# A two-layer decoder trunk: sums at the entry of each FFN made by accumulating transfers, the last covered tiles finished in a given order, four covered tiles in the second FFN

## The chip, the cores and the metric

The kernel runs on one core of a Trainium2 chip. The metric is the device time of one launch in microseconds (us). Runs are compared on the same chip, and a verdict against the kernel before is given with an interval where several rounds were run.

The engines, as the profile names them: PE is the matrix engine (TensorE) and PEld its weight loads; DVE (VectorE) and ACT (ScalarE) work on tiles of 128 partitions; POOL (GpSimd) and SP (SyncE) issue transfers here. A transfer that POOL issues can add what it carries onto its target in SBUF ("accumulating transfer"); those of SP only copy.

## What is computed

A trunk of two layers over 512 tokens of width 1024, all in float32. The change concerns the two FFN of each layer, ffn1 and ffn2; the mixer between them is left alone.

```python
def swiglu(h, w_in, w_out):
    gate, up = jnp.split(h @ w_in, 2, axis=-1)
    return (jax.nn.silu(gate) * up) @ w_out
# per layer
x = x + 0.5 * swiglu(rms_norm(x, ffn1_norm), ffn1_w_in, ffn1_w_out)   # ffn1
x = x + mixer(rms_norm(x, mix_norm))
x = x + 0.5 * swiglu(rms_norm(x, ffn2_norm), ffn2_w_in, ffn2_w_out)   # ffn2
```

D = 1024, T = 512 tokens, and the hidden width is 2816, which is 22 tiles of 128. `w_in` holds 1024 x 5632 (gate, then up), `w_out` 2816 x 1024.

## The kernel before

Everything stands transposed: x as 8 tiles of 128 features x 512 tokens, weights as the held operand of the matmuls. Each float32 operand is split into a high and a low part ("hi", by a cast on ACT, and "lo", the rest, by a subtraction on DVE), and each product is made of three matmuls (hi·hi, hi·lo, lo·hi; `mm3`, L326, L332, L333).

**Two ways through `w_in`.** The hidden tiles are taken in pairs. The first few are "covered" (`cover`, L495): done plainly, 8 k-tiles x 4 banks x 3 matmuls of 128x512 = 96 for a pair. Their weights come in four granules per pair, which SP loads (L295) and ACT and DVE split (L314, L315). All others are done by a scheme of seven products instead of eight (`halved`, L637; a Strassen form): a unit is a pair of tiles, its weights in four quarters of 512x256 (q0, q1 the two halves of k for the gate, q2, q3 for up), x in four quarters, and each of the products P1 to P7 multiplies one combination of weight quarters with one combination of x quarters, in 24 matmuls of 128x256. The products of a unit run in the order P1, P2, P6, P5, P7, P3, P4; P1, P6, P7 and P4 accumulate onto one bank, which is copied out in between (g1 after P1, L792; g2 after P6, L799).

`covered` is 6 for ffn1 of layer 0, 4 for ffn1 of layer 1, and 6 for both ffn2 (in `trunk_kernel`, L1515 on). While the covered tiles run, everything that the first unit needs is made ready.

**The entry.** In the first covered pair the norm ends (`end_norm`, L426): `inv`, the inverse root of the mean square per token, exists then. `halves_of_x` (L576) scales x by it and by the gain (8 operations of 128x512 on DVE, L589), makes the sums of quarters that P6, P5, P7 and P4 need on DVE (L601, L607), and splits all seven parts (`part`, L614: ACT L620, DVE L621). It is a generator: two or seven parts are made during the first pair, the rest during the second.

The first unit's four quarters of weights are loaded into tiles of the pool that x's parts don't use, and DVE makes its four sums S1 to S4 (`total`, L685): S1 q2+q3, S2 = S, S3 = q0, S4 = q1. The first two are made before the covered tiles end, S3 and S4 during the first two products. For every later unit the first and the last sum are accumulating transfers on POOL (`add`, L672, from DRAM; `add_second`, L722, from the tile S). A product's weights are split three products ahead (`LEAD`, `prepare`, L687: ACT L697, DVE L699).

**What sets the order.** A scheduler orders what is not fixed; instructions passed to `follow` (L275; the short names A, V, G, S for ACT, DVE, POOL and SP) keep the order in which they are written on their engine. `plan` (L57) lists for every product which loads, sums and hidden sums are issued behind it.

**The last covered pair.** When it is done, its four banks hold gate and up of two tiles; `finish` (L547) multiplies them by `inv` (L552, L553), takes the SiLU (L269) and writes the hidden tiles (L571, L574). For the last pair this is done behind the first product (n == 0 in `ffn`, L449), in an order that the scheduler chooses.

Of the kernel before, what the change touches and what calls it, by code (L numbers as in the profile page):

```python
# [8 lines left out]
F32 = mybir.dt.float32  # L9
# [5 lines left out]
ALU = mybir.AluOpType  # L15
# [8 lines left out]
P = 128  # L24
# [25 lines left out]


SUM = {
    "P2": (1, 0), "P1": (0, 0), "P5": (0, 0), "P6": (0, 0), "P7": (0, 1), "P3": (1, 1), "P4": (0, 0),
# [3 lines left out]
def plan(covered):  # L57
# [34 lines left out]
    for u in dict.fromkeys((k, w) for k, w, _ in seq):  # L92
# [69 lines left out]
class Trunk:  # L162
# [273 lines left out]
    def ffn(self, w_in, w_out, next_gain, covered, begin=None, out=None):  # L436
# [5 lines left out]
        with tc.tile_pool(name=self.n("ffn"), bufs=1) as fp:  # L442
# [6 lines left out]
            for n, _ in enumerate(halved):  # L449

                if n == 0:
                    finish()

# [41 lines left out]
    def cover(self, fp, w_in, covered, begin, then):  # L495
# [7 lines left out]
        for f in range(0, covered, 2):  # L503
# [35 lines left out]
            def finish(f=f, banks=banks):  # L539
                for i in range(2):  # L540
                    self.finish(fp, f, i, banks[2 * i], banks[2 * i + 1])

            if f + 2 < covered:
                finish()
        return finish

    def finish(self, fp, f, i, pg, pu):  # L547
# [4 lines left out]
        nc.vector.tensor_mul(gi, pg, self.inv)  # L552
        nc.vector.tensor_mul(ui, pu, self.inv)  # L553
        self.act(gi, gi, AF.Silu)
        a, k = divmod(f + i, 4)
        for b in range(2):
            self.hidden(self.quarter(fp, 0, a, b)[:, k, :], *(t[:, 256 * b : 256 * b + 256] for t in (gi, ui)), a != b)

# [17 lines left out]
    def halves_of_x(self, fp):  # L576


        nc = self.nc
        H = T // 2  # L580
        xn = []
        self.ngain = self.const.tile([P, KD], F32, tag="ngain", name=self.n("ngain"))
        nc.scalar.activation(self.ngain, self.gain, AF.Copy, scale=-1.0)
        for q in range(4):
            xq = fp.tile([P, 2, T], F32, tag=f"r{q + 2}", name=self.n("xn"))
            for i in range(2):
                k = 2 * q + i

                nc.vector.scalar_tensor_tensor(  # L589
                    out=xq[:, i, :], in0=self.xT[:, k, :],  # L590
                    scalar=(self.ngain if k < 4 else self.gain)[:, k : k + 1],
                    in1=self.inv, op0=ALU.mult, op1=ALU.mult,
                )
            xn.append(xq)

        quarter = lambda a, b: [xn[2 * a + i][:, :, b * H : (b + 1) * H] for i in range(2)]
        both = lambda t: [t[:, 2 * i : 2 * i + 2, :] for i in range(2)]

        def minus(out, a, b, op=ALU.subtract):
            for o, u, v in zip(out, a, b):  # L600
                nc.vector.tensor_tensor(o, u, v, op=op)  # L601
            return out

        def neither(out, a, b):

            for o, u, v in zip(out, a, b):
                nc.vector.scalar_tensor_tensor(  # L607
                    out=o, in0=u, scalar=-1.0, in1=v, op0=ALU.mult, op1=ALU.subtract
                )
            return out  # L610

        self.xc = {}

        def part(name, src):  # L614
            c = len(self.xc)
# [3 lines left out]
            for h, l, u in zip(both(hi), both(lo), src):  # L619
                nc.scalar.copy(h, u)  # L620
                nc.vector.tensor_sub(l, u, h)  # L621
            self.xc[name] = hi, lo

        b11, b12, b21, b22 = (quarter(a, b) for a in range(2) for b in range(2))
# [12 lines left out]
    def halved(self, fp, w_in, w_out, covered):  # L637
# [63 lines left out]
        def moving(c, p):  # L701

            t = self.quarter(fp, c, *SUM[p])
# [3 lines left out]
            if p in ("P1", "P7", "P4"):  # L707
                A(nc.scalar.activation(hi, t, AF.Copy, scale=-1.0))
                V(nc.vector.scalar_tensor_tensor(
                    out=lo, in0=t, scalar=-1.0, in1=hi, op0=ALU.mult, op1=ALU.subtract  # L710
                ))
            else:
                A(nc.scalar.copy(hi, t))
                V(nc.vector.tensor_sub(lo, t, hi))
            mov[c, p] = hi, lo
# [27 lines left out]

        tags = {0: "03", 1: "51", 2: "42"}
        self.hh, self.hl = [], []
# [23 lines left out]
        for n, (kind, w, p) in enumerate(seq):  # L769
# [747 lines left out]
def trunk_kernel(  # L1517
# [6 lines left out]
    for l in range(DEPTH):  # L1524
# [41 lines left out]
```

## Time and profile before

| | us |
|---|---|
| median of 3 runs | 1871.98 |
| lowest, highest | 1868.59, 1883.21 |
| the profiled execution | 1880.58 |
| its span, first to last instruction | 1878.8 |
| mean granted clock of PE | 0.996 of full |
| PE busy | 1848.1 (98%) |
| DVE busy | 1480.0 (79%) |
| ACT busy | 1002.6 (53%) |
| POOL busy | 163.6 (9%) |

How the views read. A line of the timeline has the start, the duration, the engine, the line of the kernel, the operation, out<-in, the operand sizes, and in brackets how long the engine was idle before it and what released it. A list of waits has: who waits <- for whom: us in all, how often, longest. A window line has the stretch (us from the span's start), its length, the busy us and the number of instructions of each engine, the granted clock (1.00 is full), the share of DMA that was busy, and GB/s. "hl" are split weights, "xc" x's parts, "w" raw weights of a unit, "S" its sum, "st" a granule. The stages of the four FFN that matter, by the first weight load of each:

| | covered pairs | first product | g2 waited for at |
|---|---|---|---|
| ffn1, layer 0 | three | 81.4 | 95.19 |
| ffn2, layer 0 | 606.9, 629.5, 653.3 | 675.0 | 689.04 |
| ffn1, layer 1 | two, the last from 963.95 | 985.7 | 999.64 |
| ffn2, layer 1 | three | 1596.8 | 1610.05 |

### The profile page before, as it was taken

Reading aid. Unit: us, or ns where it says so; the run is one execution under the profiler, and the core shown is the slowest. Engines: PE = TensorE matmul, PEld = TensorE weight load, DVE = VectorE, ACT = ScalarE, POOL = GpSimd, SP = SyncE. Lnnn points to the kernel's source line nnn. Section 1 sums busy time; section 2 is a strip of 40 time slices with the busy share of each in tenths; the row PEclk is TensorE's granted clock in tenths of the full one; section 3 lists DMA queues with packets and bytes.
Section 4 is the critical chain, followed back from the end, with each engine's and each line's share of the span. In section 5 each row is a group of like instructions: output and inputs, shape, how many; then the busy total and the mean of one; then the engine's idle time right before and its main releaser. Section 6 shows DMA issues by size and latency. Waiting matters only on the chain. (4 is left out here: it accounts for less than half of the span.)

```text
span 1878.8 us, 33066 instructions
## 1 busy us (share of the span) xinstructions
PE 1848.1 (98%) x13384; PEld 1711.3 (91%) x13384; DVE 1480.0 (79%) x2117; ACT 1002.6 (53%) x1483; POOL 163.6 (9%) x170
## 2 busy tenths in 40 slices
PE   8999999999999999999999999999999999999999
PEld 6899999899878789999889999988998777999997
DVE  7978886677887868879687887867768878787783
ACT  4455554564676535555455555545547663545552
POOL 0011120100000001112000111201000000020210
PEclk9999999999999999999999999999999999999999
DMA  5658783232323367868255786813223235577762
GB/s 146 179 137 190 181 179 91 73 92 68 79 79 96 100 172 176 182 169 169 79 155 149 168 190 170 169 62 93 81 65 86 80 99 156 159 148 189 150 131 90
DMA packets 241513, 245.60 MB, mean 131 GB/s; under 512 B 19504, under 2 KB 226864, under 8 KB 241360
## 3 DMA queue, kind: packets, MB, share of 16 engines
q1 hardware_dynamic: 191792, 183.69, 32.2%
q0 software_dynamic: 49568, 59.79, 19.9%
q8 instruction: 105, 1.72, 0.4%
q14 instruction: 48, 0.39, 0.1%
HBM read 220.83 MB, written 2.10 MB: 119 GB/s over the span
## 5 line engine op out<-in xcount | busy, mean ns | idle before, releaser
L697 ACT CAST hl<-w 128x1024 fp32r<-128x1024 f32 x310 | 325.0, 1049 | 352.1 <-PE mm L333 94.1
L699 DVE TENSOR_TENSOR hl<-w,hl 128x1024 fp32r<-128x1024 f32 x310 | 378.6, 1222 | 103.3 <-ACT hl L697 103.0
L326 PE MATMUL mm<-xc,hl 128*128 128x256 f32 (+1 forms) x1011 | 282.6, 280 | 6.9 <-ACT g L799 6.9
L333 PE MATMUL mm<-xc,hl 128*128 128x256 f32 x1008 | 282.3, 280 | 0.0
L332 PE MATMUL mm<-xc,hl 128*128 128x256 f32 x1008 | 282.1, 280 | 0.0
L315 DVE TENSOR_TENSOR hl<-st,hl 128x512 fp32r<-128x512 f32 (+2 forms) x204 | 176.4, 866 | 114.9 <-ACT hl L314 113.6
L314 ACT CAST hl<-st 128x512 fp32r<-128x512 f32 (+2 forms) x204 | 154.9, 762 | 192.8 <-PE mm L333 65.7
L326 PEld LDWEIGHTS mm<-xc,hl 128*128 128x128 f32 x1011 | 192.0, 190 | 7.8 <-ACT g L799 7.5
L333 PEld LDWEIGHTS mm<-xc,hl 128*128 128x128 f32 x1008 | 192.7, 191 | 0.2
L332 PEld LDWEIGHTS mm<-xc,hl 128*128 128x128 f32 x1008 | 191.7, 190 | 0.0
L326 PE MATMUL mm<-hl,x 128*128 128x256 f32 (+1 forms) x384 | 112.6, 293 | 0.7 <-DVE ft L420 0.4
L326 PE MATMUL mm<-x,hl 128*128 128x512 f32 x272 | 109.2, 401 | 0.0
L333 PE MATMUL mm<-hl,x 128*128 128x256 f32 (+1 forms) x384 | 107.7, 281 | 0.0
L332 PE MATMUL mm<-hl,x 128*128 128x256 f32 (+1 forms) x384 | 107.5, 280 | 0.0
L333 PE MATMUL mm<-x,hl 128*128 128x512 f32 x272 | 106.5, 391 | 0.0
L332 PE MATMUL mm<-x,hl 128*128 128x512 f32 x272 | 106.0, 390 | 0.0
L333 PE MATMUL sc<-m,hl 128*128 128x256 f32 x336 | 93.6, 279 | 0.0
L332 PE MATMUL sc<-m,hl 128*128 128x256 f32 x336 | 93.4, 278 | 0.0
L326 PE MATMUL sc<-m,hl 128*128 128x256 f32 x336 | 93.4, 278 | 0.0
L326 PE MATMUL po<-xc,hl 128*128 128x256 f32 x336 | 93.4, 278 | 0.0
L332 PE MATMUL po<-xc,hl 128*128 128x256 f32 x336 | 93.4, 278 | 0.0
L333 PE MATMUL po<-xc,hl 128*128 128x256 f32 x336 | 93.4, 278 | 0.0
(474 smaller groups left out, 5515.8 us busy)
## 6 DMA issues: line engine op xcount, KB each, us to landing
w<-in_ffn_w_in_dram SPq DMA_DIRECT2D x132, 512.0 KB, 5.1
w<-in_ffn_w_out_dram SPq DMA_DIRECT2D x64, 512.0 KB, 4.4
w<-in_ffn_w_out_dram POOLq DMA_DIRECT2D x56, 512.0 KB, 8.4
st<-in_ffn_w_in_dram SPq DMA_DIRECT2D x88, 256.0 KB, 3.1
st<-in_w_mix_in_dram SPq DMA_DIRECT2D x88, 256.0 KB, 2.7
w<-in_ffn_w_in_dram POOLq DMA_DIRECT2D x29, 512.0 KB, 8.1
w<-S POOLq DMA_DIRECT2D x29, 512.0 KB, 4.8
st<-in_ffn_w_out_dram SPq DMA_DIRECT2D x24, 512.0 KB, 3.5
```

Of the source, the lines that this page charges most:

```text
L314: a = nc.scalar.copy(hi, src[:, c : c + w])
L315: b = nc.vector.tensor_sub(lo, src[:, c : c + w], hi)
L326: i = nc.tensor.matmul(acc[:, c], ah, bh[:, c], start=first and c.start == 0, stop=False, skip_group_check=True,)
L332: nc.tensor.matmul(acc, ah, bl, start=False, stop=False, skip_group_check=True)
L333: i = nc.tensor.matmul(acc, al, bh, start=False, stop=last, skip_group_check=True)
L697: A(nc.scalar.copy(hi, src))
L699: return lambda: V(nc.vector.tensor_sub(lo, src, hi))
```

## The change

1. *x's sums.* `halves_of_x` scales x by quarters (16 operations of 128x256 in place of 8 of 128x512), and the sums of quarters are made by four accumulating transfers on POOL, SBUF to SBUF: a: (0,0)+=(0,1), b: (0,1)+=(1,1), c: (0,0)+=(1,1), d: (0,0)+=(1,0), of 512 KB each. The signs that DVE's subtractions had are put into the gain and into the split (`two`, for `NEGATIVE`). Each part is split in one piece of 128x1024. The parts come in the order P1, P2, P3, P5, P6, P7, P4.
2. *The first unit.* Its quarters are loaded by SP in the order q2, q0, q3, q1 into tiles of their own, and a fifth load puts q2 into S as well. POOL then adds q3 onto q2, q0 onto S and q3 onto S; q0+=q2 and q1+=S come later, as for other units. The four sums on DVE are gone.
3. *The last covered pair* is finished one tile behind the second product and one behind the fourth, in the given order. Its gate tile uses the buffers of g2 instead of g1. `halved` yields once more, so that the loads go ahead of the last pair but one.
4. *Small ones.* g1 is now g1 - acc (the sign moved), and one Square is put in the order of the activation tables.
5. *ffn2 has four covered tiles* instead of six, so one more unit of the seven products.

```diff
+NEGATIVE = ("P1", "P7", "P4")
...
             if w == covered:
-                begin = {0: -5, 1: -4, 2: -3, 3: -2}
-                when(-1, 9, "total", u, "S1")
-                when(-1, 9, "total", u, "S2")
-                when(0, 2, "total", u, "S3")
-                when(1, 2, "total", u, "S4")
+                when(-1, 5, "add", u, 0, 2)
+                when(-1, 6, "adds", u)
+                continue
...
-        nc.scalar.activation(t, r, AF.Square)
+        self.act(t, r, AF.Square)
...
-                if n == 0:
-                    finish()
+                if n in (1, 3):
+                    finish(n // 2)
...
-            if f + 2 == covered:
+            if f + 4 == covered or f + 2 == covered:
                 next(then)
...
-        gi = fp.tile([P, T], F32, tag="g1", name=self.n("gi"), bufs=2)
+        gi = fp.tile([P, T], F32, tag="g2", name=self.n("gi"), bufs=2)
...
+        A, V = ((lambda i, e=e: self.follow(e, i)) if keep else (lambda i: i) for e in "av")
+        V(nc.vector.tensor_mul(gi, pg, self.inv))
+        V(nc.vector.tensor_mul(ui, pu, self.inv))
+        A(self.act(gi, gi, AF.Silu))
...
-        yield part("P1", b11)
-        yield part("P2", b21)
-        t1 = both(fp.tile([P, 4, H], F32, tag="S", name=self.n("T"), bufs=2))
-        minus(t1, b12, b11)
-        t2 = minus(b11, b22, t1, ALU.add)
-        yield part("P6", t2)
-        yield part("P5", t1)
-        yield part("P7", neither(b12, b12, b22))
-        yield part("P3", b22)
-        yield part("P4", minus(b21, b21, t2))
+        add = lambda x, y: nc.gpsimd.dma_start(q(*x), q(*y), accum_op=ALU.add)
...
+        yield part("P1")
+        add((0, 0), (0, 1))
+        yield part("P2")
+        yield part("P3")
+        yield part("P5")
+        add((0, 0), (1, 1))
+        add((0, 1), (1, 1))
+        yield part("P6")
+        add((0, 0), (1, 0))
+        yield part("P7")
+        yield part("P4")
...
-        first = [x for x in steps[-1] if x[0] == "total"]
-        steps[-1] = [x for x in steps[-1] if x[0] != "total"]
-        run(-1)
+        u = seq[0][:2]
+        for q in (2, 0, 3, 1):
+            raw[u, q] = t = fp.tile(
+                [P, 4, 2 * P], F32, tag=("mh", "ml")[q % 2], name=self.n("w"), bufs=2
+            )
+            S(nc.sync.dma_start(t, src(u, q)))
+        sums[u] = fp.tile([P, 4, 2 * P], F32, tag="S", name=self.n("S"), bufs=2)
+        S(nc.sync.dma_start(sums[u], src(u, 2)))
+        add(u, 2, 3)
+        for q in (0, 3):
+            G(nc.gpsimd.dma_start(sums[u], src(u, q), accum_op=ALU.add))
+        yield
         for s in seq[: LEAD - 1]:
             prepare(*s)()
+        run(-1)
         yield
-        for _, args in first:
-            total(*args)
         prepare(*seq[LEAD - 1])()
...
-                V(nc.vector.tensor_add(g1, g1, acc))
+                V(nc.vector.tensor_sub(g1, g1, acc))
...
         k.ffn(
-            ffn2_w_in[l], ffn2_w_out[l], ffn1_norm[l + 1] if l + 1 < DEPTH else None, 6,
+            ffn2_w_in[l], ffn2_w_out[l], ffn1_norm[l + 1] if l + 1 < DEPTH else None, 4,
```

In the built kernel POOL's order at each entry is q2+=q3, S+=q0, S+=q3, a, b, c, and then, in ffn2, q0+=q2, q1+=S, d, and in ffn1 d, q0+=q2, q1+=S. In ffn2 SP's five loads stand behind the third granule of the last covered pair. ACT has the split of P4's x part ahead of the g1 copy.

More of the change, by code (lines that the diff above doesn't have):

```diff
@@ L618, in part, with two @@
             )
-            for h, l, u in zip(both(hi), both(lo), src):
-                nc.scalar.copy(h, u)
-                nc.vector.tensor_sub(l, u, h)
+            self.two(hi, lo, src, name in NEGATIVE)
             self.xc[name] = hi, lo
-        b11, b12, b21, b22 = (quarter(a, b) for a in range(2) for b in range(2))
-        yield part("P1", b11)
-        yield part("P2", b21)
-        t1 = both(fp.tile([P, 4, H], F32, tag="S", name=self.n("T"), bufs=2))
-        minus(t1, b12, b11)
-        t2 = minus(b11, b22, t1, ALU.add)
-        yield part("P6", t2)
-        yield part("P5", t1)
-        yield part("P7", neither(b12, b12, b22))
-        yield part("P3", b22)
-        yield part("P4", minus(b21, b21, t2))
+        yield part("P1")
[9 more added lines that the diff above has]
+        yield part("P4")
+    def two(self, hi, lo, src, other):
+        nc = self.nc
+        if other:
+            return (
+                nc.scalar.activation(hi, src, AF.Copy, scale=-1.0),
+                nc.vector.scalar_tensor_tensor(
+                    out=lo, in0=src, scalar=-1.0, in1=hi, op0=ALU.mult, op1=ALU.subtract
+                ),
+            )
+        return nc.scalar.copy(hi, src), nc.vector.tensor_sub(lo, src, hi)
     def halved(self, fp, w_in, w_out, covered):
@@ L701, in moving @@
         def moving(c, p):
-            t = self.quarter(fp, c, *SUM[p])
             hi, lo = (
@@ L706, in moving @@
             )
[L707 to L714, printed above, removed]
+            a, v = self.two(hi, lo, self.quarter(fp, c, *SUM[p]), p in NEGATIVE)
+            A(a), V(v)
             mov[c, p] = hi, lo
@@ L742, in halved @@
         pair = lambda t: t.rearrange("p (i t) -> p i t", i=2)
-        tags = {0: "03", 1: "51", 2: "42"}
+        tags = {0: (0, 3), 1: (5, 1), 2: (4, 2)}
         self.hh, self.hl = [], []
@@ L750, in run @@
                 do[name](*args)
-        first = [x for x in steps[-1] if x[0] == "total"]
-        steps[-1] = [x for x in steps[-1] if x[0] != "total"]
-        run(-1)
+        u = seq[0][:2]
+        for q in (2, 0, 3, 1):
+            raw[u, q] = t = fp.tile(
+                [P, 4, 2 * P], F32, tag=("mh", "ml")[q % 2], name=self.n("w"), bufs=2
+            )
+            S(nc.sync.dma_start(t, src(u, q)))
[5 more added lines that the diff above has]
+        yield
         for s in seq[: LEAD - 1]:
             prepare(*s)()
+        run(-1)
         yield
-        for _, args in first:
-            total(*args)
         prepare(*seq[LEAD - 1])()
```

50 lines of the change are left out of this document (18 added, 32 removed).

## The prediction

> **What bounds the kernel now.** I read the busy shares first, then the list of waits of TensorE's weight loads, then the instructions around the waits that stand alone, and last the busy time by stretches.
>
> ```profile
> span 1878.8 us, 33066 instructions
> PE 1848.1 (98%) x13384; PEld 1711.3 (91%) x13384; DVE 1480.0 (79%) x2117; ACT 1002.6 (53%) x1483; POOL 163.6 (9%) x170
> PEld mm L326 <- ACT g L799: 7.5, 3, 2.9
> PEld sc L326 <- ACT xc L620: 3.7, 2, 1.8
> PEld sc L326 <- ACT g L799: 2.8, 1, 2.8
> ```
>
> PE is busy 98% of the span, so only three things move the time: matmuls fewer or more, idle gaps of PE, and the clock it is granted. The rows of the waits read: who waits, for whom, us in all, how often, longest. The g2 copy (L799) makes four gaps, one at each FFN's entry; the split of x (L620) makes two, in the two ffn2. These six are what the change touches. Here is ffn2 of layer 0: weight loads, then the two other engines, then stretches (from:to, length, busy us of PE, PEld, DVE, ACT, POOL with instruction counts, granted clock, DMA share, GB/s).
>
> ```profile
> 651.27 0.19 PEld L333 LDWEIGHTS po<-x,hl 128*128 128x128 f32 x1
> 653.30 0.19 PEld L326 LDWEIGHTS sc<-x,hl 128*128 128x128 f32 x1 [1.84 <-ACT xc L620]
> 674.99 0.19 PEld L326 LDWEIGHTS mm<-xc,hl 128*128 128x128 f32 x1
> 686.00 0.19 PEld L333 LDWEIGHTS mm<-xc,hl 128*128 128x128 f32 x1
> 689.04 0.19 PEld L326 LDWEIGHTS mm<-xc,hl 128*128 128x128 f32 x1 [2.86 <-ACT g L799]
> ```
> ```profile
> 687.45 1.04 ACT L697 CAST hl<-w 128x1024 fp32r<-128x1024 f32 x1 [2.30 <-DVE w L685]
> 688.40 0.59 ACT L799 ACTIVATE g<-mm 128x512 f32<-128x512 f32 x1
> 686.15 1.22 DVE L685 TENSOR_TENSOR w<-w,S 128x1024 f32<-128x1024 f32 x1
> ```
> ```profile
> 653.30:675.00 21.70, 21.67 (x96) 17.95 (x97) 13.46 (x22) 6.28 (x9) 1.34 (x1) 1.00 0.67 203
> 675.00:685.90 10.90, 10.90 (x97) 10.86 (x96) 10.31 (x15) 5.45 (x7) 0.00 (x0) 1.00 0.65 178
> 686.00:693.27 7.27, 4.61 (x27) 4.41 (x26) 3.82 (x4) 2.97 (x4) 0.00 (x0) 0.77 0.51 159
> 689.50:693.00 3.50, 3.50 (x19) 3.50 (x18) 1.48 (x2) 0.93 (x2) 0.00 (x0) 0.51 0.52 163
> ```
>
> A covered pair takes 21.70. Four products take 10.90, so one takes 2.72 and a pair in seven products 19.1. The fifth product waits for g2, which stands on ACT behind a weight split, which waited for the first unit's last sum on DVE (686.15 to 687.37). It takes 7.27 where 2.72 are due: 4.55 lost, of it 2.86 waiting and 1.7 because the clock stood at 0.51 for 3.5 us behind the wait (3.5 x 0.49). Behind the shorter wait at 651.27 the next 96 matmuls ran at clock 1.00, so a gap of 1.84 costs itself only (2.03 from load to load).
>
> **The change part by part.** *Four covered tiles in ffn2.* Per ffn2 21.70 - 19.1 = 2.6 of PE go, and the wait at 653.30, which stood ahead of the third pair, must be looked for elsewhere: the products now begin at 651.3, when they are ready, instead of 675.0. *First unit's sums off DVE.* S1 to S4 leave DVE, and so does what made g2 late. The other entries:
>
> ```profile
> 95.19 0.19 PEld L326 LDWEIGHTS mm<-xc,hl 128*128 128x128 f32 x1 [2.61 <-ACT g L799]
> 999.64 0.19 PEld L326 LDWEIGHTS sc<-xc,hl 128*128 128x128 f32 x1 [2.77 <-ACT g L799]
> 1610.05 0.19 PEld L326 LDWEIGHTS mm<-xc,hl 128*128 128x128 f32 x1 [2.06 <-ACT g L799]
> ```
>
> With 1.7 of clock each they are worth 4.3 (ffn1, layer 0), 4.5 (ffn1, layer 1) and 3.8 (ffn2, layer 1). The price of 1.7 rests on a clock that halves after waits of this length; the Trainium skill ("TensorE: Matmul & The Clock Gate", Part 1 on the clock gate) puts the limit at idle gaps above some 3.4 us. The stretch at 0.51 after a wait of 2.86 contradicts that; by the page the four waits were worth their 10.3 alone, not 17.2, and the sum would come out 7 higher at the entries and lower where I charge new waits.
>
> *What takes their place.* The queue of POOL now carries, per entry: q2+=q3, S+=q0, S+=q3, the four sums of x (a to d), q0+=q2, q1+=S. In ffn2 the order is q2+=q3, S+=q0, S+=q3, a, b, c, q0+=q2, q1+=S, d; in ffn1 a to d stand ahead of the last two. S+=q3 waits until S+=q0 has landed, and everything behind waits with it. The rows for such transfers: issues on POOL, then from issue to landing.
>
> ```profile
> 105.33 0.90 POOL L722 DMA_DIRECT2D w<-S  x1 [31.08 <-DVE hl L699]
> 105.88 1.67 POOL L672 DMA_DIRECT2D w<-in_ffn_w_in_dram  x1
> ```
> ```profile
> w<-S POOLq DMA_DIRECT2D x1, 512.0 KB, 4.7
> w<-in_ffn_w_in_dram POOLq DMA_DIRECT2D x1, 512.0 KB, 7.6
> ```
> ```profile
> w<-in_ffn_w_in_dram POOLq DMA_DIRECT2D x29, 512.0 KB, 8.1
> w<-S POOLq DMA_DIRECT2D x29, 512.0 KB, 4.8
> ```
> ```profile
> DMA to landing us min/median/max: 5.5/8.2/15.0
> ```
> ```profile
> DMA to landing us min/median/max: 4.5/4.8/6.3
> ```
>
> The two last are for L672 (from DRAM) and L722 (from SBUF). The pair at 105 lands at 110.0 and 113.5: a transfer issued right behind another comes about 3.3 later. I take 7.6 for one from DRAM that starts alone, 4.8 for one from SBUF, 3.3 for one behind another; ends 5.5 and 8.4, 4.5 and 6.3. 7.6 because the entries are full of weight loads; the third pair's stretch shows the load:
>
> ```profile
> GB/s 0 59 203 413 164 0 0 0 39 231 374 226 205 300 238 180 247 280 347 339 162 252 334 385 392 279 293 300 297 138 141 195 206 180 175 254 300 313 367 303
> w<-in_ffn_w_in_dram POOLq DMA_DIRECT2D x1, 512.0 KB, 8.4
> ```
>
> *ffn2, layer 0.* When can the five loads of the first unit start? They stand on SP behind a wait for DVE's last squared-sum addition (L414), 622.54 + 0.68:
>
> ```profile
> 622.54 0.68 DVE L414 TENSOR_TENSOR sqa<-sqa,sq 128x512 f32<-128x512 f32 x1
> L697 ACT CAST hl<-w 128x1024 fp32r<-128x1024 f32 x310 | 325.0, 1049 | 352.1 <-PE mm L333 94.1
> L699 DVE TENSOR_TENSOR hl<-w,hl 128x1024 fp32r<-128x1024 f32 x310 | 378.6, 1222 | 103.3 <-ACT hl L697 103.0
> 682.47 0.42 DVE L571 SCALAR_TENSOR_TENSOR hq<-gi,ui 128x256 f32<-128x256 f32 x1
> 683.74 0.68 DVE L552 TENSOR_TENSOR gi<-pt,inv 128x512 f32<-128x512 f32 x1
> ```
>
> Five of 0.52 MB at some 290 GB/s (an estimate from the busy slices above) and two us of way: S lands at 635. S+=q0 635 to 642.6; S+=q3, issued 0.5 later, 650.7; copy a 3.3 behind it, about 654. Then P5's x part: ACT 1.05, DVE 1.22, 656.3. DVE's queue holds two hidden tiles and a product behind that (2 x 0.42 + 0.68), then P1's weight split (1.22): 659. The first product is due at 651.3 and starts at 659: 7.7 late. ACT's queue is behind the same part, and has the copies for P7, P6 and P4 of x ahead of the g1 copy; P6 accumulates onto P1's bank and so needs that copy. Copy c, which waits for P5's split, lands at 662.4; q0+=q2, which waits for P1's split, 659.3 to 666.9; q1+=S 3.3 later, copy d another 3.2: 673.3. P4's part 1.05, a weight split 1.05, g1 0.59: 676. P6, the third product, runs 676 to 680.6 (2.72 + 1.7 for the clock), and should have ended at 651.3 + 3 x 2.72 = 659.5: 21.1 late. After that everything has landed. So this entry takes 21.1 + 19.1 = 40.2 from 651.3, against 2.0 + 21.7 + 4.55 = 28.3 before: **+11.9**. In layer 1, with 27.5 before, **+12.7**.
>
> *ffn1, layer 1.* Here are four covered tiles before and after, and the last pair ran
>
> ```profile
> 963.95:985.70 21.75, 21.75 (x98) 18.01 (x97) 21.75 (x35) 10.94 (x17) 1.32 (x1) 1.00 0.76 215
> 947.61 0.69 DVE L414 TENSOR_TENSOR sqa<-sqa,sq 128x512 f32<-128x512 f32 x1
> ```
>
> The loads go at 948.3, S lands at 960 (11.7 as above), the two sums at 967.6 and 975.7, copy a at 978.9. ACT has P5's part ahead of the split of the last of the pair's four granules; with a SiLU between and DVE's 1.22 that granule is ready at 984, due at 985.7 - 21.75/4 = 980.3. Lost: 3.7 + 1.7. Copy c waits for P5's split and d for P6's, a transfer of 4.8 and two splits each: d lands at 995, P4's part and P2's weights behind it (1.05 + 1.05 + 1.22) let the second product start at 998.7, 4.6 after the first (991.4 + 2.72) ended: lost 4.6 + 1.7. Together 11.7 against the 4.5 that go: **+7.2**.
>
> *ffn1, layer 0.* The same order, but the weights come in the kernel's first 20 us and x is whole far ahead of the products; I find every transfer landing before the entry: **-4.3**.
>
> *The rest at nothing.* Sixteen scalings of x at 0.42 for eight at 0.68 add 1.3 to DVE under a covered pair, where it is idle most (13.46 of 21.70). The last pair's finish in two halves is hidden under seven products, since their banks are other ones; if it were not, it costs its 0.68 twice. The sign of g1 and the place of one Square change no duration.
>
> Sum: 11.9 + 12.7 + 7.2 - 4.3 = **+27.5**. The profiled execution, 1880.6 us with its span of 1878.8, would become 1908; the median of the three runs is 1872, and 1872 + 27.5 is some **1900**.
>
> **The rivals.** *The transfers meet little traffic* (5.6 from DRAM, 3.2 behind). For: ffn2 loads fewer granules than before in this stretch. Against: five loads more, and 8.4 in the stretch quoted. Sums at 640.6 and 646.7, a at 649.9, first product 654.9, q0+=q2 660.9, d 667.3, g1 670, P6's end 674.5, 15 late: +5.8 and +6.5; in ffn1, layer 1, copy a is in time and only P2 waits, about 7.4, +2.9; with -4.3 it is +11: 1883.
>
> *All transfers cost like the lowest from SBUF*, 4.5, as if the source and the accumulation counted for nothing: sums 639.5 and 644.5, a 647.7, first product some 1.5 late, c 654.5, P6's split 658.8, d 663.3, g1 666: 9.3 + 1.7 late, +1.8 and +2.5; ffn1, layer 1, -2; in all -2: 1870. Against it: 5.5 is the lowest of the transfers from DRAM. The Trainium skill ("DMA: Bandwidth & Descriptors", "Anatomy of one DMA — SWDGE (gpsimd) path") goes further, 2.0 us and the bytes at 436 GB/s, 3.2 for 512 KB, by which I would estimate about 1860; no transfer of the trace is that short.
>
> *All is ahead of the products* (the faster side). Then four waits (4.55 + 4.5 + 4.3 + 3.8) and in each ffn2 2.03 and 2.6 go: -26.4, 1846. It decides at copy a landing by 645 and d by 653, that is with loads that start some 10 us earlier than the addition at 622.54 lets them.
>
> *Worse*: at 8.4 and 6.3 throughout, the chain of five in ffn2 is some 7 longer, +44 in all: 1916.
>
> **How the numbers follow.** Chances: forecast 0.56, worse 0.05, little traffic 0.23, lowest rows 0.08, all ahead 0.08. One per cent, about what a measurement here can tell, is 18.7 us: slower by that are the forecast and the worse, 0.61; within it the two next, 0.31; faster 0.08. The forecast's own range by the bounds of the transfers is 1890 to 1914; down to 1874 it takes in the case of little traffic and leaves out lowest rows, all ahead and half of the worse, under 0.2.
>
> **What would show it.** Right: in both ffn2 a wait of PE ahead of the first product of 5 to 9 us and one ahead of the third of 10 to 16, with ACT's P4 part of x or the g1 copy as releaser; no wait at L799; S+=q3 landing near 650 and copy d near 673; the clock at half behind each. In ffn1, layer 1, a wait inside the last covered pair and one at the second product. Wrong: if S+=q3 lands before 643, or if the g1 copy does not stand behind copy d, nearly all of the +25 of the two ffn2 is gone.

## The result, and the profile after

| | median of 4 runs, us | lowest, highest |
|---|---|---|
| before | 1870.28 | 1864.67, 1883.21 |
| after | 1933.88 | 1917.16, 1943.38 |

The ratio is 1.032, 95% interval 1.023 to 1.041: slower, by 63.6 between the medians where 27.5 was forecast. The profiled execution after took 1933.97 against 1880.58, 53.4 more. First the head of the page after and its waits of the weight loads (who waits <- for whom: us in all, how often, longest):

```profile
span 1932.2 us, 33422 instructions
PE 1862.2 (96%) x13528; PEld 1730.9 (90%) x13528; DVE 1456.8 (75%) x2077; ACT 1009.3 (52%) x1467; POOL 206.9 (11%) x210
```
```profile
PEld sc L334 <- DVE hl L698: 21.6, 3, 10.9
PEld sc L327 <- ACT g L792: 16.3, 2, 8.3
PEld mm L327 <- ACT hl L696: 9.8, 3, 5.1
```

Line numbers have moved: L327 and L334 are the first and the third matmul of a split product, L698 and L696 the low and high split of weights, L792 the g1 copy, L600 the copies a to d, L754 the sums onto S. The g2 copy is gone from the list, and the six old waits with it. Three groups stand in their place, in the order of the lines: the first product of each ffn2 waits for P1's weights, its third for g1, and in both ffn1 the second product for P2's weights. Here are the first two in ffn2 of layer 0, from the timeline of the weight loads:

```profile
673.89 0.29 PEld L334 LDWEIGHTS sc<-xc,hl 128*128 128x128 f32 x1 [10.87 <-DVE hl L698]
689.95 0.29 PEld L327 LDWEIGHTS sc<-xc,hl 128*128 128x128 f32 x1 [7.98 <-ACT g L792]
```

Behind them, POOL's queue (start, duration of the issue), the time from issue to landing of its transfers (last number; the two onto S, a, and d, in their order), and ACT:

```profile
644.77 1.28 POOL L754 DMA_DIRECT2D S<-in_ffn_w_in_dram  x1 [3.72 <-DMA S<-in_ffn_w_in_dram]
655.23 1.29 POOL L754 DMA_DIRECT2D S<-in_ffn_w_in_dram  x1 [9.18 <-DMA S<-in_ffn_w_in_dram]
655.98 1.46 POOL L600 DMA_DIRECT2D xn<-xn  x1
680.09 0.86 POOL L600 DMA_DIRECT2D xn<-xn  x1 [0.25 <-DVE xc L634]
```
```profile
S<-in_ffn_w_in_dram POOLq DMA_DIRECT2D x1, 512.0 KB, 10.2
S<-in_ffn_w_in_dram POOLq DMA_DIRECT2D x1, 512.0 KB, 10.9
xn<-xn POOLq DMA_DIRECT2D x1, 512.0 KB, 13.1
xn<-xn POOLq DMA_DIRECT2D x1, 512.0 KB, 7.3
```
```profile
669.13 1.04 ACT L634 CAST xc<-xn 128x1024 fp32r<-128x1024 f32 x1 [16.04 <-DMA xn<-xn]
687.41 1.06 ACT L629 ACTIVATE xc<-xn 128x1024 fp32r<-128x1024 f32 x1 [8.43 <-DMA xn<-xn]
688.37 1.03 ACT L696 CAST hl<-w 128x1024 fp32r<-128x1024 f32 x1
689.31 0.59 ACT L792 ACTIVATE g<-sc 128x512 f32<-128x512 f32 x1
```

The chain can be read off: the second sum starts when the first has landed (644.77 + 10.2), copy a stands behind it and lands at 669.1, ACT sits idle for 16 us in front of P5's part, and everything queued behind that part is late. Then the same once more with d, P4's part and g1.

A second thing is in no list of waits. Stretches of 20 us in the middle of the products (length, busy us of PE, PEld, DVE, ACT, POOL with counts, clock, DMA share, GB/s), after:

```profile
150.00:170.00 20.00, 20.00 (x172) 20.00 (x171) 18.76 (x21) 10.59 (x12) 4.84 (x5) 1.00 0.82 167
740.00:760.00 20.00, 20.00 (x179) 20.00 (x178) 15.65 (x17) 8.99 (x11) 3.53 (x3) 1.00 0.54 119
```

PE is busy throughout and its clock is 1.00 in both, yet 172 matmuls fall into one and 179 into the other (the two or three that overlap the edges counted in): from start to start it is about 118 ns ("the longer step" from here on) against 113.4. One rate holds from one wait to the next. After, both ffn1 ran at the longer step nearly to their end, 8.7 and 9.5 us each; before, ffn2 of layer 1 did, 8.4, and the tail of ffn1 of layer 0.

So that the two are kept apart, the steps from one weight load to the next are summed by FFN, over the products and the 26 us ahead of them: what exceeds 113.4 ns (226.7 in covered pairs) counts as a wait when the step is over 400 ns, as half clock between 170 and 400, and as the longer step below 170.

| us: wait, half clock, longer step | before | after |
|---|---|---|
| ffn1, layer 0 | 2.7, 2.0, 0.9 | 4.5, 2.6, 8.7 |
| ffn2, layer 0 | 4.7, 1.9, 0.0 | 19.0, 4.5, 0.1 |
| ffn1, layer 1 | 3.2, 1.8, 0.0 | 12.0, 3.1, 9.5 |
| ffn2, layer 1 | 3.9, 1.6, 8.4 | 19.4, 4.3, 1.0 |
| waits and half clock, sum | 21.8 | 69.4 |
| longer step, sum | 9.3 | 19.3 |

Waits and half clock +47.6, longer steps +10.0, matmuls saved 5.3 (21.70 - 19.05 in each ffn2): +52.3 of the 53.4.

### The profile page after: what moved, and what is told of

The parts are those of the page before. It is cut to its first block, busy times and chain, and to the rows that moved or that the text cites. A ratio compares the mean times of both kernels' runs of the same rounds, so it can differ in the third digit from the quotient of the medians.

```text
span 1932.2 us, 33422 instructions
## 1 busy us (share of the span) xinstructions
PE 1862.2 (96%) x13528; PEld 1730.9 (90%) x13528; DVE 1456.8 (75%) x2077; ACT 1009.3 (52%) x1467; POOL 206.9 (11%) x210
## 4 chain that ended last, share of the span: by engine, by line
PE 82%; DMA 7%; DVE 5%; ACT 3%; issue 3%; POOL 0%; SPq 0%; ACTq 0%; POOLq 0%; DVEq 0%
PE mm L327 12%; PE mm L334 12%; PE mm L333 12%; PE sc L327 6%; PE sc L333 6%; PE sc L334 5%; PE pt L327 5%; PE pt L333 5%; PE pt L334 5%; DMA xn<-xn 3%; PE po L327 3%; PE po L333 3%; PE po L334 3%; DMA S<-in_ffn_w_in_dram 1%; DVE hl L316 1%
## 5 line engine op out<-in xcount | busy, mean ns | idle before, releaser
L696 ACT CAST hl<-w 128x1024 fp32r<-128x1024 f32 x322 | 337.5, 1049 | 346.8 <-PE mm L334 93.9
L698 DVE TENSOR_TENSOR hl<-w,hl 128x1024 fp32r<-128x1024 f32 x322 | 393.3, 1222 | 101.9 <-ACT hl L696 101.3
L327 PE MATMUL mm<-xc,hl 128*128 128x256 f32 (+1 forms) x730 | 207.7, 285 | 8.9 <-ACT hl L696 8.9
L334 PE MATMUL mm<-xc,hl 128*128 128x256 f32 x728 | 207.8, 285 | 2.6 <-DVE hl L698 2.6
L333 PE MATMUL mm<-xc,hl 128*128 128x256 f32 x728 | 207.4, 285 | 0.0
L334 PE MATMUL sc<-xc,hl 128*128 128x256 f32 x528 | 150.3, 285 | 21.0 <-DVE hl L698 21.0
L327 PE MATMUL sc<-xc,hl 128*128 128x256 f32 (+1 forms) x530 | 150.2, 284 | 15.9 <-ACT g L792 15.9
L327 PEld LDWEIGHTS mm<-xc,hl 128*128 128x128 f32 x730 | 141.3, 194 | 9.8 <-ACT hl L696 9.8
L333 PE MATMUL sc<-xc,hl 128*128 128x256 f32 x528 | 149.7, 284 | 0.0
L334 PEld LDWEIGHTS mm<-xc,hl 128*128 128x128 f32 x728 | 139.5, 192 | 3.4 <-DVE hl L698 3.4
L333 PEld LDWEIGHTS mm<-xc,hl 128*128 128x128 f32 x728 | 141.2, 194 | 0.0
L327 PE MATMUL pt<-xc,hl 128*128 128x256 f32 x480 | 132.6, 276 | 0.0
L333 PE MATMUL pt<-xc,hl 128*128 128x256 f32 x480 | 132.6, 276 | 0.0
L334 PE MATMUL pt<-xc,hl 128*128 128x256 f32 x480 | 132.6, 276 | 0.0
L334 PEld LDWEIGHTS sc<-xc,hl 128*128 128x128 f32 x528 | 103.2, 195 | 21.6 <-DVE hl L698 21.6
L327 PEld LDWEIGHTS sc<-xc,hl 128*128 128x128 f32 x530 | 103.6, 195 | 16.4 <-ACT g L792 16.3
L327 PE MATMUL mm<-hl,x 128*128 128x256 f32 (+1 forms) x384 | 112.2, 292 | 0.7 <-DVE ft L421 0.4
L327 PE MATMUL mm<-x,hl 128*128 128x512 f32 x272 | 109.8, 404 | 0.0
L334 PE MATMUL mm<-hl,x 128*128 128x256 f32 (+1 forms) x384 | 107.3, 279 | 0.0
```

What stands on the lines that cost most here:

```text
L327: i = nc.tensor.matmul(acc[:, c], ah, bh[:, c], start=first and c.start == 0, stop=False, skip_group_check=True,)
L333: nc.tensor.matmul(acc, ah, bl, start=False, stop=False, skip_group_check=True)
L334: i = nc.tensor.matmul(acc, al, bh, start=False, stop=last, skip_group_check=True)
L696: A(nc.scalar.copy(hi, src))
L698: return lambda: V(nc.vector.tensor_sub(lo, src, hi))
```

## The experiments

The same sums, and the medians, for all of them. "Ratio" is against the kernel before on the same chip (its medians there 1874 to 1877).

| | median, us | ratio (95%) | waits and half clock | longer step |
|---|---|---|---|---|
| e1 after, six covered | 1904.04 | 1.013 (1.007 to 1.019) | 24.9 | 18.1 |
| e2 after, x on DVE | 1882.40 | 1.002 (0.999 to 1.005) | 29.3 | 19.3 |
| e3 before, four covered | 1878.09 | 1.000 (0.997 to 1.004) | 29.9 | 18.4 |
| e4 before, given order | 1880.44 | 1.003 (0.9995 to 1.006) | 14.0 | 17.7 |
| e5 after, S on DVE | 1903.97 | 1.015 (1.010 to 1.020) | 50.8 | 9.9 |
| e6 after, P4 late | 1912.93 | 1.021 (1.017 to 1.025) | 60.1 | 9.2 |
| e7 before, g2 first | 1864.40 | 0.994 (0.992 to 0.997) | 7.7 | 9.1 |
| e8 after again | 1924.47 | 1.026 (1.022 to 1.030) | 69.4 | 9.8 |
| e9 after, held loads | 1928.51 | 1.027 (1.020 to 1.034) | 67.2 | 10.7 |
| e10 after, x on DVE, six | 1855.86 | 0.988 (0.982 to 0.994) | 5.3 | 0.9 |
| e11 as e10, g2 and u2 first | 1870.86 | 0.995 (0.991 to 0.998) | 4.1 | 9.7 |
| e12 before, g2 and u2 first | 1858.98 | 0.989 (0.984 to 0.994) | 5.9 | 0.7 |

The account closes: 1871.3 (the profiled execution before without its longer steps), plus the change of both columns, less 5.3 where four tiles are covered in ffn2, gives each profiled time within 1.3 us; for e1, with the 11.6 of its covered pairs added, within 2.1.

**e1, six covered tiles in ffn2.**

```diff
-            ffn2_w_in[l], ffn2_w_out[l], ffn1_norm[l + 1] if l + 1 < DEPTH else None, 4,
+            ffn2_w_in[l], ffn2_w_out[l], ffn1_norm[l + 1] if l + 1 < DEPTH else None, 6,
```

> The changed kernel with six covered tiles in ffn2 again; all else as changed. In the changed kernel's trace S+=q3 lands 3 to 4 us behind the due time of the first product of ffn2, copy d 20 behind it. Theory 1, the chain of transfers is too long for four covered tiles: with 21.7 us more ahead of the first product the two waits of ffn2 (10.9 and 8.0 of PE, clock 4.4 beside) fall to below 3 us each, 2.6 of matmuls come back per ffn2: 1934 - 47 + 5, some 1892. Rival, the waits hang on the order on ACT and DVE and move along with the products: ffn2 keeps over 12 us of waits, 1925 or more. Either way each FFN that ends its last wait at a step of 118 ns from matmul to matmul instead of 113.4 has 8 to 9 us more, so one such stage up or down moves these figures by 9.

Median 1904, 12 above the first theory's 1892. The waits of 10.9 and 8.0 went, as that theory says. But in the second covered pair of each ffn2 some 5.8 us of waits came up; weight loads and DVE there:

```profile
669.82 0.29 PEld L327 LDWEIGHTS pt<-x,hl 128*128 128x128 f32 x1 [5.11 <-DVE ui L555]
```
```profile
667.94 1.23 DVE L630 SCALAR_TENSOR_TENSOR xc<-xn,xc 128x1024 fp32r<-128x1024 f32 x1 [3.81 <-ACT xc L629]
669.08 0.68 DVE L555 TENSOR_TENSOR ui<-pt,inv 128x512 f32<-128x512 f32 x1
```

In DVE's queue the split of a part of x (L630), which waits for a copy, stands ahead of the read of a bank (L555) that PE wants for the next pair, and that read starts only behind it. The copies do harm even where the cover is long.

**e2, x's sums on DVE.** The part `halves_of_x` is that of the kernel before. P2's part has the other sign then, and its product is subtracted as in the changed kernel, so one term of the gate has the wrong sign; the instructions and their shapes are the same. With the copies go the split of each part in one piece and the new order of the parts; the three were not tried apart.

> The changed kernel with x's sums on DVE as before (halves_of_x of the kernel before); the first unit's sums stay transfers, four covered tiles stay. Theory 1, the copies a to d make most of the waits: ffn2's wait at the first product (10.9) and at the third (8.0) fall together below 7 per ffn2, the third product now waiting for S+=q3 alone; ffn1 of layer 0 has no wait over 1 us, ffn1 of layer 1 less than 4 of its 12: about 1890. Rival, the sums onto S are to blame alone: the third product waits for S as long as now and the first still over 5, 1915 or more. Second rival, DVE is too full with x's sums when only four tiles are covered: a wait of over 8 us for DVE ahead of the first product, 1915 or more.

Median 1882: 42 to 52 less than the changed kernel. ffn1 of layer 0 has no wait left. In ffn2 the first product waits little, and the second, P2, whose weights are S, waits for the split of S (the third was expected to):

```profile
648.07 0.29 PEld L334 LDWEIGHTS sc<-xc,hl 128*128 128x128 f32 x1 [2.46 <-DVE hl L713]
658.96 0.28 PEld L334 LDWEIGHTS sc<-xc,hl 128*128 128x128 f32 x1 [6.67 <-DVE hl L713]
```

More than the 7 in sum that was expected (9.1 and 10.9), and the profiled execution, 1891.9, has 19.3 of longer steps in it; without them it would lie at 1873, where the kernel before would lie at 1871. So the copies of x, with what is queued behind them, make most of the loss; the sums onto S are late by themselves in ffn2 with four covered tiles, and e10 below shows no such wait with six.

**e3, four covered tiles alone**, in the kernel before, by the same edit as e1's in the other direction.

> The kernel before with four covered tiles in ffn2 and nothing else of the change. If the four covered tiles are worth their matmuls, 2 x 2.6, and the sums on DVE come in time: 1865. If DVE, busy 21.73 of 21.80 us in the second pair, can't have x's parts and the first unit's sums ready 21.7 us earlier: waits of 3 to 8 us at the first products of each ffn2, 1872 to 1885. If any kernel with four covered tiles waits as the changed one does: 19 us of waits per ffn2, 1900 or more.

Median 1878, ratio 1.000: the middle case. A wait of 3.7 for the split of P1's weights on DVE at the first product eats the matmuls saved and the old bank wait.

**e4, the finish in the given order alone**, in the kernel before: the edit of the diff above in `ffn`, `cover` and `finish`.

> The kernel before with the last covered pair finished in two halves behind the second and the fourth product, in the given order, and nothing else of the change. The wait for g2 (2.06 to 2.86 us at four entries, 10.3 in all, and 1.7 each at half clock) stands behind DVE's fourth sum. If that sum is late because the finish of the last pair is ahead of it on DVE: all four waits below 1 us, 1870 - 13 to 17, some 1855, and since no wait is left every product at 113.4 ns a matmul. If the sum is late for another reason (S3, the splits): waits as before, 1870 within 5.

Median 1880, 3 above the kernel before: no gain, and the second case comes nearest. g2 still waits, but partly for something new: ACT, and the weight load that it lets go:

```profile
683.11 0.63 ACT L269 ACTIVATE gi<-gi 128x512 f32<-128x512 f32 x1 [2.50 <-DVE gi L553]
```
```profile
685.22 0.19 PEld L326 LDWEIGHTS mm<-xc,hl 128*128 128x128 f32 x1 [1.88 <-ACT g L800]
```

The order puts a SiLU of the covered tile, which waits for DVE, ahead of the g2 copy. The waits are a little shorter and cost hardly any half clock (14.0 for 21.8), but in the profiled execution both ffn2 were left at the longer step, which took as much again.

**e5, S made on DVE**, x's sums still transfers.

```diff
-        S(nc.sync.dma_start(sums[u], src(u, 2)))
         add(u, 2, 3)
-        for q in (0, 3):
-            G(nc.gpsimd.dma_start(sums[u], src(u, q), accum_op=ALU.add))
         yield
+        total(u, "S2")
```

> The changed kernel with the first unit's S made by one addition on DVE (S = q0 + (q2+q3), 1.22 us) in place of the fifth load and the two accumulating transfers; x's sums stay transfers, four covered tiles stay. Theory 1, the transfers S+=q0 and S+=q3, each waiting for the one before, are what holds copy a back to 669: a then stands behind q2+=q3 alone, lands some 12 to 18 us earlier, the wait of 10.9 at ffn2's first product falls below 2, and the one of 8.0 at the third below 5, since d comes earlier too; ffn1 of layer 1 loses its wait inside the covered pair: 1890 to 1900. Rival, the four copies of x are too long by themselves: over 12 us of waits are left per ffn2, 1915 or more.

Median 1904, 20 to 30 less than the changed kernel, between the two cases. Copy a landed at 657.7 instead of 669.1, 11 earlier; the waits in ffn2 of layer 0 fell to

```profile
669.52 0.29 PEld L334 LDWEIGHTS sc<-xc,hl 128*128 128x128 f32 x1 [6.52 <-DVE hl L698]
681.09 0.29 PEld L327 LDWEIGHTS sc<-xc,hl 128*128 128x128 f32 x1 [4.47 <-ACT g L789]
```

not below 2. Copy a itself now waits for the split of P1's part on DVE and starts at 649.3, so the chain of S was only part of its lateness. And a is no longer what the first product waits for: it landed some 5 us before that product began. On DVE the split of P1's weights (L698) now stands behind that of P7's part (L630), which waits for the next copy, b:

```profile
665.35 1.06 ACT L629 ACTIVATE xc<-xn 128x1024 fp32r<-128x1024 f32 x1 [5.54 <-DMA xn<-xn]
666.44 1.23 DVE L630 SCALAR_TENSOR_TENSOR xc<-xn,xc 128x1024 fp32r<-128x1024 f32 x1 [4.02 <-ACT xc L629]
668.25 1.22 DVE L698 TENSOR_TENSOR hl<-w,hl 128x1024 fp32r<-128x1024 f32 x1
```

**e6, P4's part behind g1.**

```diff
+                if n == 0:
+                    for _ in self.xparts:
+                        pass
...
+            a, v = self.two(hi, lo, src, name in NEGATIVE)
+            if name == "P4":
+                self.follow("a", a)
+                self.follow("v", v)
```

> The changed kernel with the part P4 of x split behind the first product's g1 copy, in the given order on ACT and DVE; every transfer stays where it is. Theory 1, what waits in the entry is not P4's product (the seventh) but the work queued behind P4's part on ACT: the waits at P2 in ffn1 go (3.2 + 1.05 in layer 0, 5.1 + 0.96 in layer 1, and 2.6 and 3.1 of clock), the one at the third product of ffn2 (8.0) falls below 3, where S itself is waited for; the one at the first product (10.9, copy a) stays: 1934 - 28 to 38. Rival, the products wait for the late copies anyway: new waits at the fourth to seventh products, 1925 or more.

Median 1913, between the two cases. The six other parts are made ahead, and `xparts` has P4's left. In ffn1 of layer 0 waits and half clock fell from 7.1 to 2.3, and in ffn2 the third product no longer waits for g1. But two products on there is a wait of the same size (weight load, and ACT before it):

```profile
679.71 0.29 PEld L327 LDWEIGHTS sc<-xc,hl 128*128 128x128 f32 x1 [7.32 <-ACT g L805]
```
```profile
672.92 1.06 ACT L635 ACTIVATE xc<-xn 128x1024 fp32r<-128x1024 f32 x1 [6.89 <-DMA xn<-xn]
679.07 0.59 ACT L805 ACTIVATE g<-sc 128x512 f32<-128x512 f32 x1
```

P4's part still waits for copy d in ACT's queue, now ahead of g2. Both theories had a share: the queue makes the wait, and moving the part hands it to the next in the queue.

**e7, the g2 copy first**, in the kernel before.

```diff
+            if n == 2:
+                work[u, "g2"] = g2 = tmp("g2")
+                A(nc.scalar.activation(g2, acc, AF.Copy, scale=-1.0))
             rest = prepare(*seq[n + LEAD]) if n + LEAD < len(seq) else None
...
+            elif p == "P6" and n == 2:
+                pass
```

> The kernel before with one instruction moved: in the first unit of each FFN the copy of g2 stands ahead of the split of P3's weights on ACT instead of behind it. If g2 waits only for its place behind that split (which waits for DVE's fourth sum): the four waits of 2.06 to 2.86 and the 1.7 each at half clock are gone, -13 to -17 against the kernel before, and with no wait left inside the products every stage runs at 113.4 ns a matmul, which saves the 8 to 9 us of a stage that a wait left at 118: 1850 to 1862. If P3's weights are late themselves: a wait of 0.5 to 2 us two products later, -5 to -10.

Median 1864, 10 less than before. The four waits went; 0.4 to 1.0 came at the sixth product, not for P3's weights as the second case had it, but for u2. One of these left ffn1 of layer 0 at the longer step.

**e8, the changed kernel again.**

> The changed kernel once more, unchanged. In its first profile the products ran at 118 ns from matmul to matmul in both ffn1 (8.7 and 9.5 us in all) and at 113.4 in both ffn2, and changed between the two only at a wait. If a wait leaves it at one or the other by chance: the same waits within 0.5 us, but another set of slow stages, and a time of 1915 and 8 to 9.5 for each slow stage. If code or addresses decide: the same two stages, 1934 within 3.

Median 1924. Waits and half clock sum to 69.4 as before, single waits within 1.2, but the longer step is in another place; stretches of this run:

```profile
150.00:170.00 20.00, 20.00 (x179) 20.00 (x179) 19.19 (x20) 10.90 (x12) 5.93 (x5) 1.00 0.88 171
1700.00:1720.00 20.00, 20.00 (x172) 20.00 (x171) 17.20 (x18) 9.92 (x11) 3.85 (x3) 1.00 0.82 183
```

ffn1 of layer 0 has 179 here where it had 172, and ffn2 of layer 1 has 172 where it had 179 (longer steps 1.0 there before, 9.5 now). It is the same program on the same data, so the code alone does not decide. Its four times are 1915.3 and three of 1924.3 to 1924.7, one such stage apart.

**e9, later loads held back.**

```diff
+        if covered == 4:
+            held = fp.tile([P, 1], F32, tag="held", name=self.n("held"))
+            S(nc.sync.dma_start(held, sums[u][:, 0, 0:1]))
```

> The changed kernel, with SP's loads of the second and later units held back (where four tiles are covered) until S is complete: one transfer of a column of S on SP stands ahead of them. If the sums took 10 to 13 us in ffn2 because those loads fill the transfer engines beside them (share of busy engines 1.1 to 1.2 there): S+=q0 at 8 or less instead of 10.1, S+=q3 at 8 or less instead of 11.2, copy a lands 5 to 8 us earlier, and the wait at ffn2's first product falls from 10.9 to 3 to 6; the held loads may be missed later. If such transfers are that long by themselves: the wait stays at 10 to 11.7.

Median 1929. First the stretches of the two sums onto S in the changed kernel, then that of the second sum here, the landing times of its two sums and of a, and its weight loads:

```profile
644.50:654.90 10.40, 10.40 (x48) 8.61 (x47) 9.72 (x16) 4.20 (x5) 1.28 (x1) 1.00 1.17 267
654.90:666.10 11.20, 8.31 (x39) 6.75 (x37) 0.00 (x0) 0.00 (x0) 2.21 (x2) 1.00 1.14 291
```
```profile
644.90:650.60 5.70, 5.70 (x27) 4.72 (x26) 1.58 (x3) 0.00 (x0) 2.21 (x2) 1.00 0.82 151
```
```profile
S<-in_ffn_w_in_dram POOLq DMA_DIRECT2D x1, 512.0 KB, 8.0
S<-in_ffn_w_in_dram POOLq DMA_DIRECT2D x1, 512.0 KB, 5.7
xn<-xn POOLq DMA_DIRECT2D x1, 512.0 KB, 7.5
```
```profile
657.93 0.19 PEld L334 LDWEIGHTS sc<-xc,hl 128*128 128x128 f32 x1 [3.11 <-DVE hl L698]
679.50 0.29 PEld L327 LDWEIGHTS sc<-xc,hl 128*128 128x128 f32 x1 [9.48 <-ACT g L795]
```

With SP's loads away the second sum took 5.7 instead of 10.9, a 7.5 instead of 13.1, and the first wait fell from 10.87 to 3.11, as expected of contention. The share alone does not set the time, though: the first sum here took 8.0 in a stretch with a share of 1.20. The held loads then ran into the later copies, and the wait for g1 grew to 9.48: the total stayed. In the changed kernel the share is above 1.1 for the 20 us shown here, and holding the loads back only chose which transfer was late.

**e10, x's sums on DVE and six covered tiles**: e1's and e2's edits, and g1 + P2 again as before.

> The changed kernel with x's sums on DVE as before and six covered tiles in ffn2; of the change only the first unit's sums by transfers and the finish in the given order are left (P2 is added to g1 again, as x's parts have their old signs). If the copies of x and the short cover made all of the loss, and the sums of weights by transfers are worth something when they have time: no wait over 2 us at any entry of an FFN, no half clock in ffn2, -10 to -17 against the kernel before, 1858 to 1865. If the sums onto S are late even so: waits of 3 us or more at the third product in ffn2, 1870 or more.

Median 1856, ratio 0.988: it beats both kernels. Waits and half clock are 5.3 in all; of the waits inside the products only ffn1 of layer 1 has some over 0.2 (1.0 and 1.7). The wait ahead of ffn2's third pair is 0.6 instead of 1.84.

**e11, e10 with g2 and u2 first.** The edit is e7's with n in (2, 3), for g2 and u2.

> As the run before, and the first unit's copies of g2 and u2 ahead of the weight splits that stand ahead of them on ACT. If then no wait is left in the products, all four stages run at 113.4 ns a matmul in every execution: 1846 to 1856, and the spread of the runs below 6 us. If a wait at the entry is left that is not g2's or u2's: like the run before.

A miss: median 1871, and a spread of 22 (1856 to 1879). The two waits of e10 went, but each of the four FFN got one of 0.42 at the seventh, which by the times in the timeline follows DVE's addition onto u2 behind the finish of the covered tiles (the profile names no releaser). 0.42 us costs little by itself; the profile has one stage at the longer step, 8.9 us, and the runs lie 0 to 22 above the lowest.

**e12, the kernel before with g2 and u2 first.** The same edit in the kernel before.

> The kernel before with the first unit's copies of g2 and of u2 ahead of the splits of P3's and P4's weights on ACT. With g2 alone moved, waits of 0.4 to 1.0 for u2 were left at the sixth product of each FFN, and one of them left its stage at 118. If u2 waited for its place only: these go, every stage at 113.4: 1850 to 1858, and a spread below 6 us. If P3's weights or the fourth sum are late themselves: a wait of up to 1 us stays and some executions keep a slow stage: 1858 to 1865.

Median 1859: three runs at 1854.6 to 1855.7, three at 1862.3 to 1864.4. One wait of 0.18 and one of 0.47 are left inside the products. So the second expectation fits.

## Why the prediction came out as it did

- **Right: the places and the order of cause.** The forecast had ffn2's first product wait for P1's weights behind P5's part and copy a, and its third for g1 behind P4's part and d; both stand in the trace with these releasers. e2 (no copies) and e9 (shorter transfers) move them as that chain says. The g2 wait went, as forecast.
- **Mis-sized: the transfers.** "I take 7.6 for one from DRAM that starts alone": in ffn2 of layer 0 the sums onto S took 10.2 and 10.9. The stage began 11.0 later than in the kernel before (its last squared-sum addition at 633.53 for 622.54). With that taken off, S landed at 633.7 (635 in the forecast), S+=q3 at 655.1 (650.7), a at 658.1 (654) and d at 676.4 (673.3). e9 shows why: the loads for later units ran beside the sums, at a DMA share of 1.14 to 1.17; the row of 7.6 was taken at 0.93. "4.8 for one from SBUF": in ffn1 of layer 1, where the sums took 7.5 each, near the 7.6 taken, c and d took 6.4 and 8.1. So the entries came to +14.3 (forecast 11.9) and +15.6 (12.7) in ffn2 and +10.1 (7.2) in ffn1 of layer 1, by waits and half clock less the matmuls. The split of the waits was off too: 10.9 and 8.0 in ffn2 of layer 0, where 7.7 and 11.6 (676 less the end of the second product, 659 + 2 x 2.72) follow from the forecast. The half clock behind the first wait, which was not charged, takes up part of the second. (676 + 2.72 + 1.7 is 680.4, not 680.6; 0.2 changes nothing.)
- **Wrong: ffn1 of layer 0.** "I find every transfer landing before the entry" failed. Weight load, POOL, landing of d, and ACT there:

```profile
89.08 0.19 PEld L327 LDWEIGHTS mm<-xc,hl 128*128 128x128 f32 x1 [3.21 <-ACT hl L696]
```
```profile
79.03 0.86 POOL L600 DMA_DIRECT2D xn<-xn  x1 [9.08 <-DVE xc L634]
```
```profile
xn<-xn POOLq DMA_DIRECT2D x1, 512.0 KB, 8.0
```
```profile
87.04 1.06 ACT L629 ACTIVATE xc<-xn 128x1024 fp32r<-128x1024 f32 x1 [8.09 <-DMA xn<-xn]
88.00 1.03 ACT L696 CAST hl<-w 128x1024 fp32r<-128x1024 f32 x1
```

  The weights were early, but the copies wait for one another through the splits of x: a, P5's split, c, P6's split, d. The last starts at 79.0, lands at 87.0, and P2's weights stand behind P4's part. e6, which moves only that part, takes 4.8 of the 7.1 away. In place of -4.3 it was +2.4.
- **Missing: what a wait does to the rate afterwards.** The sum charged a wait with itself and 1.7 of half clock. That the products may go on 4% slower for the rest of the FFN was in no term; it is +10.0 between the two profiles. So of the 24.8 between the forecast's 27.5 and the 52.3 found, these steps are 10.0, ffn1 of layer 0 is 6.7, and the three other entries, where transfers came later than taken, are about 8. By the account a changed kernel without the longer step would take 1913.6; its lowest times, not profiled, are 1915 and 1917. The first median, 1934, lies above the second, 1924, by about one such stage, and which executions have how many is chance as far as the runs show.
- **The rivals.** Little traffic and lowest rows fell: the transfers were longer, not shorter. All ahead fell, too. The worst case named the right direction, 8.4 and 6.3 throughout. Its +44 is near the +42.3 that waits, half clock and saved matmuls came to (47.6 less 5.3), but that is luck in part: it kept ffn1 of layer 0 at -4.3, and its bound of 8.4 was itself passed in ffn2 of layer 0.
- **The Trainium skill's price** for a software transfer ("DMA: Bandwidth & Descriptors", "Anatomy of one DMA — SWDGE (gpsimd) path"), 3.2 us by my estimate for 512 KB, is not met by the accumulating transfers here: 4.5 is the shortest of L722's in the kernel before, and those onto S took 5.7 at a DMA share of 0.82, 8.0 at 1.20, and 10.2 and 10.9 at 1.17 and 1.14.

## What to carry to other kernels

A sum moved from a compute engine to a transfer is only free if nothing in an in-order queue waits for it: count what stands behind the first instruction that waits on it, and price the transfer at the load of that stretch, not at its median. Try a change's parts singly: here one part (the first unit's sums by transfers, with six tiles covered and x left on DVE) together with the finish in a given order gained 1.2%, while x's sums by transfers cost more than everything else gave. But look for the smallest edit first: e12, two copies put further ahead on ACT in the kernel before, gained 1.1% without any of the change, so the 1.2% shows that the g2 wait is worth removing and not that the transfers are needed for it. And a kernel whose main engine is 98% busy should be looked at for the rate of its instructions as well as for its gaps.

## What the runs showed of the hardware

- **Two rates of matmul at the same granted clock.** Steps of 113.4 and about 118 ns between matmuls of 128x256. In 14 profiles with 56 FFN, none of the 9 with no wait over 0.2 us inside the products ran at the longer step for its greater part; of the 47 with one, 17 did. The rate changed only at a wait, even at one of 0.06 us or 0.4 us. What decides it at a wait is not shown.
- **The granted clock changes in slots of 3.41 us.** In each of the 14 profiles all its changes lie whole multiples of 3.413 us apart. In the kernel before, the half clock behind the four waits begins at 95.62, 689.54, 1000.15 and 1611.14 and lasts one slot each, which is the 1.7 that the prediction charged (3.41 x 0.5). How long a single wait is does not decide: one of 2.00 us in e4 was followed by a slot at half clock, one of 2.46 in e2 was not, and two of 1.44 and 1.38 in one slot of the changed kernel were. Weight loads, then the slots in question, for the changed kernel with the slot of the waits ahead (clock third from the right):

```profile
93.86 0.19 PEld L326 LDWEIGHTS mm<-xc,hl 128*128 128x128 f32 x1 [2.00 <-ACT g L800]
1581.41 0.19 PEld L334 LDWEIGHTS sc<-xc,hl 128*128 128x128 f32 x1 [2.46 <-DVE hl L713]
1014.73 0.30 PEld L327 LDWEIGHTS mm<-xc,hl 128*128 128x128 f32 x2 [1.44 <-ACT hl L696]
1016.52 0.19 PEld L334 LDWEIGHTS mm<-xc,hl 128*128 128x128 f32 x1 [1.38 <-DVE hl L698]
```
```profile
94.34:97.75 3.41, 3.41 (x19) 3.41 (x18) 3.17 (x6) 1.52 (x3) 0.00 (x0) 0.50 0.52 163
1582.94:1586.35 3.41, 1.46 (x13) 1.26 (x12) 0.00 (x0) 0.00 (x0) 1.84 (x2) 1.00 1.10 252
1014.23:1017.64 3.41, 1.73 (x12) 1.53 (x13) 2.24 (x3) 0.45 (x1) 1.53 (x2) 1.00 1.09 364
1017.64:1021.05 3.41, 3.03 (x15) 2.73 (x13) 0.00 (x0) 0.00 (x0) 0.65 (x1) 0.50 1.11 314
```

  Over the 14 profiles, PE was busy for 0.54 or less of every slot behind which the clock fell, and for 0.45 or more of every slot behind which it stayed at full. The Trainium skill ("TensorE: Matmul & The Clock Gate", Part 1) asks for no idle gap above some 3.4 us; shorter waits halved the clock here. The same part has a free-running window of 3413 ns; the slots of 3.413 us agree with it.
